# A hybrid decoder layer: the weights of the feature chunks stand at another place in their tiles

## Chip, cores, metric

One core of a Trainium2 chip runs the whole layer. The metric is the device time of one execution in microseconds.

## What is computed

One decoder layer on 256 tokens of width 1024, all in float32:

```python
u = rms_norm(x, attn_pre_norm)
q, k, v, x_lru, g_lru, gate_attn, gate_lru = split(u @ w_in)        # seven parts of 1024 columns
y_attn = moba_attention(rope(q), rope(k), v) @ w_branch_attn        # 8 heads of 128, causal
y_lru  = (rg_lru(conv4(x_lru)) * gelu(g_lru)) @ w_branch_lru        # recurrent branch, w_rg_a, w_rg_i
x = x + rms_norm((sigmoid(gate_attn) * y_attn + sigmoid(gate_lru) * y_lru) @ w_out)
x = x + rms_norm(square(relu(rms_norm(x) @ w_mlp_up)) @ w_mlp_down) # 1024 -> 4096 -> 1024
```

With 256 tokens the attention has one block of keys, so it is plain causal attention.

## The kernel before

**Every product is three matmuls.** Weights and features are split into a high part (rounded to the matmul's own 32-bit format) and a low part (what is left). A product is high x high, high x low and low x high, added up in one PSUM bank. `three` (L179) issues them: L180 multiplies the high weights with the high features, L181 the high weights with the low features, L182 the low weights with the high features. Each of them loads its weights anew.

**Weights come in 74 chunks** of 128 x 2048 numbers (1 MB), in one fixed order. `load` (L88) brings a chunk into one of three `wraw` tiles with a DMA from SyncE's queue. `split` (L104) makes the high part from it on ScalarE (L117), or on VectorE for chunks 17 to 22 (L115, `HI_ON_VECTOR`), and the low part on VectorE (L118, raw minus high). The parts go to tiles `whi` and `wlo`, three of each. `ahead` (L123) keeps the loads up to four chunks and the splits up to two chunks in front of the products; the splits have high priority in the order of their engines.

**Two kinds of chunks.** In a *feature chunk* the weights are what is loaded into TensorE (128 x 128 blocks), and the features stream past it, 256 columns at a time (all tokens). `feat_chunk` (L201) issues 2 x 8 x 3 = 48 matmuls for one; the first chunk has a function of its own (L191), and the two gate matrices of the recurrent branch have their own loop (L337). There are 48 feature chunks: chunks 0, 2, 4 and 6 (x_lru), 8 to 37 (q, k, the recurrent gates, three gate projections, the two branch projections) and 44 to 57 (up projection). In a *token product* it is the other way round: the features are loaded, and 512 columns of weights stream past. These are the chunks 1, 3, 5 and 7 (v, L233 to L235), 38 to 41 (`w_out`, L495 to L497), 42 and 43 (first 512 columns of the up projection, L602 to L604) and 58 to 73 (down projection, L495 to L497 again).

**Where the operands stand.** A `whi` or `wlo` tile has 2048 + 64 columns (`W_STEP`, L41 and L96). `weight_tiles` (L95) gives a slice of 2048 columns of it, which begins at the columns that the table `OFFSET` (L45) names: the first number is for the high part, the second for the low part, and a chunk that the table does not name begins at column 0. The table names all feature chunks and none of the token products. The tiles `gap_...` (`GAPS`, L40) only take up room. In the program as it is laid out, the tiles of the features (`xgh`, `xgl`, `xch`, `xcl`, `ath`, `atl`, `lrh`, `lrl`, `u2_12`, `u2_3`) and all of `whi` and `wlo` begin 32 columns past a multiple of 64 columns in their partition: `xgh` at byte 46208, the first `whi` at 161152, the first `wlo` at 186496. Blocks inside a tile start at multiples of 128 columns. So a slice that begins at column 0 of its tile stands at the place of the features modulo 64 columns, and one that begins at column 48 stands 48 columns past it, or 16 short of the next such place.

**The order of the work.** The four x_lru chunks and the four v chunks alternate in the opening, while the loads arrive. Then come q and k, the recurrent gates, the three gate projections (L435) with the heads of the attention stepped between them (`attention_step`, small matmuls L387 to L412), the branch projections (L461, L467), `w_out` with the post norm, the first up columns by tokens with transposes (L613), 14 feature chunks of the up projection (L626) and the down projection. Between two `feat_chunk` calls TensorE only waits for what `ahead` and the PSUM banks make it wait for.

Of the kernel before, what the change touches and what calls it, by code (L numbers as in the profile page):

```python
# [41 lines left out]

OFFSET = {c: (48, 16) for c in (*range(0, 8, 2), *range(8, 38), *range(44, 58))}  # L45


@with_exitstack
def hybrid_layer(ctx: ExitStack, tc: tile.TileContext, head_d, x_d, w_d, cst_d, gp_d, out_d):
# [45 lines left out]
    def weight_tiles(c):  # L95
        hi = whi_p.tile([P, 2048 + W_STEP], F32R, tag="whi", name=f"whi{c}")  # L96
        lo = wlo_p.tile([P, 2048 + W_STEP], F32R, tag="wlo", name=f"wlo{c}")
        h, l = OFFSET.get(c, (0, 0))
        return hi[:, h:h + 2048], lo[:, l:l + 2048]
# [637 lines left out]
```

## Time and profile before

| | |
|---|---|
| time, median of 3 runs | 442.46 us (442.3 to 617.95) |
| time of the profiled execution | 443.12 us |
| its span, first to last instruction | 441.3 us |
| busy: TensorE matmuls, weight loads | 429.0 us, 402.0 us |
| busy: VectorE, ScalarE, GpSimd | 293.1 us, 239.7 us, 20.7 us |
| mean granted TensorE clock | 0.996 of full speed |

The profile is one execution, recorded instruction by instruction. PE is TensorE's matmuls, PEld its weight loads, which run beside matmuls; DVE is VectorE, ACT ScalarE, POOL GpSimd, SP SyncE. The duration of a matmul is the time it is in flight: matmuls overlap, so the sum of durations is more than the time, and the distance between the starts of two neighbours is the better measure of their cost. L180 means line 180 of the kernel. PEclk is the share of TensorE's full clock that was granted.

### The profile page before, as it was taken

The numbers are of one execution on the slowest core, as the hardware profiler recorded it, in microseconds if no ns is written. First come the engines' busy times: TensorE is split into PE (matmuls) and PEld (weight loads), VectorE is DVE, ScalarE is ACT, GpSimd is POOL, SyncE is SP. The second block draws the span as 40 slices with busy tenths as digits, with TensorE's granted clock in tenths as the row PEclk, the third lists the DMA queues.
The fourth block names the chain that finished last, engine by engine and source line by source line (L and its number), as shares of the span: only waits on it lengthen the run. The fifth ranks groups of instructions, "written<-read, shape, count | busy, mean of one in ns | idle before, by whom it ended". The sixth has DMA issues, their size and how long they took to land.

```text
span 441.3 us, 7246 instructions
## 1 busy us (share of the span) xinstructions
PE 429.0 (97%) x3044; PEld 402.0 (91%) x3044; DVE 293.1 (66%) x353; ACT 239.7 (54%) x326; POOL 20.7 (5%) x48
## 2 busy tenths in 40 slices
PE   6989999999999999999999999999999999999994
PEld 6979999999999999999998879999999988888883
DVE  6749975779997666985688665666666644444424
ACT  7595753419977667553455566555555533333321
POOL 1000063202000000000000000000000000000000
PEclk9999999999999999999999999999999999999998
DMA  8968456655543455445567504555554555555202
GB/s 276 409 238 338 176 215 212 222 209 214 193 165 123 161 218 195 166 140 187 186 257 301 197 0 179 174 182 175 175 181 183 192 190 190 192 196 192 83 1 95
DMA packets 14576, 83.61 MB, mean 189 GB/s; under 512 B 1808, under 2 KB 2576, under 8 KB 5456
## 3 DMA queue, kind: packets, MB, share of 16 engines
q1 hardware_dynamic: 13520, 80.39, 50.7%
q0 software_dynamic: 736, 2.36, 1.6%
q8 instruction: 24, 0.39, 0.4%
q10 hardware_dynamic: 288, 0.39, 0.2%
q14 instruction: 8, 0.07, 0.0%
HBM read 81.04 MB, written 1.05 MB: 186 GB/s over the span
## 4 chain that ended last, share of the span: by engine, by line
PE 91%; DMA 5%; ACT 1%; DVE 1%; issue 0%; SPq 0%; DVEq 0%
PE mm L181 19%; PE mm L180 19%; PE mm L182 18%; PE acc L497 8%; PE acc L495 8%; PE acc L496 8%; DMA x_tok<-in_x_dram 2%; DMA wraw<-in_w_dram 1%; DMA xw_a<-in_head_dram 1%; PE up L604 1%; PE up L602 1%; PE v L233 1%; PE up L603 1%; PE v L234 1%; PE rg L181 1%; PE v L235 1%
## 5 line engine op out<-in xcount | busy, mean ns | idle before, releaser
L118 DVE TENSOR_TENSOR wlo<-wraw,whi 128x2048 fp32r<-128x2048 f32 (+2 forms) x78 | 163.6, 2099 | 88.3 <-ACT whi L117 87.9
L117 ACT CAST whi<-wraw 128x2048 fp32r<-128x2048 f32 (+2 forms) x72 | 125.2, 1739 | 95.8 <-PE acc L497 47.1
L180 PE MATMUL mm<-xgh,whi 128*128 128x256 f32 x384 | 107.7, 284 | 4.2 <-ACT xgh L171 4.2
L182 PE MATMUL mm<-xgh,wlo 128*128 128x256 f32 x384 | 106.6, 278 | 1.6 <-DVE wlo L118 1.6
L181 PE MATMUL mm<-xgl,whi 128*128 128x256 f32 x384 | 107.1, 280 | 0.0
L180 PEld LDWEIGHTS mm<-xgh,whi 128*128 128x128 f32 x384 | 72.2, 190 | 4.5 <-ACT xgh L171 4.2
L182 PEld LDWEIGHTS mm<-xgh,wlo 128*128 128x128 f32 x384 | 72.8, 189 | 1.8 <-DVE wlo L118 1.8
L181 PEld LDWEIGHTS mm<-xgl,whi 128*128 128x128 f32 x384 | 72.8, 189 | 0.5
L181 PE MATMUL mm<-u,whi 128*128 128x256 f32 x224 | 63.3, 283 | 0.0
L180 PE MATMUL mm<-u,whi 128*128 128x256 f32 x224 | 62.5, 279 | 0.0
L182 PE MATMUL mm<-u,wlo 128*128 128x256 f32 x224 | 62.4, 278 | 0.0
L497 PE MATMUL acc<-whi,rrl 128*128 128x512 f32 x128 | 49.8, 389 | 0.0
L496 PE MATMUL acc<-wlo,rrh 128*128 128x512 f32 x128 | 49.8, 389 | 0.0
L495 PE MATMUL acc<-whi,rrh 128*128 128x512 f32 x128 | 49.8, 389 | 0.0
L180 PEld LDWEIGHTS mm<-u,whi 128*128 128x128 f32 x224 | 42.1, 188 | 0.0
L182 PEld LDWEIGHTS mm<-u,wlo 128*128 128x128 f32 x224 | 42.0, 188 | 0.0
L181 PEld LDWEIGHTS mm<-u,whi 128*128 128x128 f32 x224 | 41.9, 187 | 0.0
L497 PEld LDWEIGHTS acc<-whi,rrl 128*128 128x128 f32 x128 | 24.0, 188 | 5.0
L496 PEld LDWEIGHTS acc<-wlo,rrh 128*128 128x128 f32 x128 | 24.0, 188 | 5.0
L495 PEld LDWEIGHTS acc<-whi,rrh 128*128 128x128 f32 x128 | 24.0, 188 | 4.9
L637 ACT CAST rrh<-rv 128x512 fp32r<-128x512 f32 x14 | 8.7, 621 | 34.6 <-DVE rv L636 34.6
L181 PE MATMUL mm<-atl,whi 128*128 128x256 f32 x64 | 18.1, 283 | 0.0
(197 smaller groups left out, 667.8 us busy)
## 6 DMA issues: line engine op xcount, KB each, us to landing
wraw<-in_w_dram SPq DMA_DIRECT2D x70, 1024.0 KB, 4.8
wraw<-in_w_dram SPq DMA_DIRECT2D x8, 256.0 KB, 6.1
xw_a<-in_head_dram SPq DMA_DIRECT2D x4, 256.0 KB, 4.3
wraw<-in_w_dram SPq DMA_DIRECT2D x2, 512.0 KB, 7.2
x_tok<-in_x_dram SPq DMA_DIRECT2D x1, 1024.0 KB, 10.5
gp<-in_gp_dram POOLq DMA_DIRECT2D x1, 1024.0 KB, 5.5
xw_b<-in_head_dram SPq DMA_DIRECT2D x3, 256.0 KB, 5.1
out_dram<-res ACTq DMA_DIRECT2D x2, 192.0 KB, 2.0
```

Of the source, the lines that this page charges most:

```text
L117: nc.scalar.copy(hi[:, k:(i + 1) * n], raw[:, k:(i + 1) * n])
L118: nc.vector.tensor_tensor(lo[:, s], raw[:, s], hi[:, s].bitcast(F32), ALU.subtract)
L180: nc.tensor.matmul(out, wh, xh, start=start, stop=False)
L181: nc.tensor.matmul(out, wh, xl, start=False, stop=False)
L182: nc.tensor.matmul(out, wl, xh, start=False, stop=stop)
L233: nc.tensor.matmul(banks[b], xgh[:, kb, s], hi[:, k, :], start=kb == 0, stop=False)
L234: nc.tensor.matmul(banks[b], xgh[:, kb, s], lo[:, k, :], start=False, stop=False)
L235: nc.tensor.matmul(banks[b], xgl[:, kb, s], hi[:, k, :], start=False, stop=kb == KB - 1)
L495: nc.tensor.matmul(out, xh[:, s], hi[:, hs], start=first, stop=False)
L496: nc.tensor.matmul(out, xh[:, s], lo[:, hs], start=False, stop=False)
L497: nc.tensor.matmul(out, xl[:, s], hi[:, hs], start=False, stop=last)
L637: nc.scalar.copy(hi, v)
```

## The change

The table `OFFSET` names the same chunks, with another pair of numbers: both parts of a feature chunk's weights begin at column 13 of their tiles, where the high part began at column 48 and the low part at column 16. Nothing else changes: not the tiles or their sizes, nor the instructions or their order. 13 columns are 52 bytes.

```diff
-OFFSET = {c: (48, 16) for c in (*range(0, 8, 2), *range(8, 38), *range(44, 58))}
+OFFSET = {c: (13, 13) for c in (*range(0, 8, 2), *range(8, 38), *range(44, 58))}
```

## Rows read from the trace of the kernel before

**Rows 1.** The page, part 1: busy us (share of the span) xinstructions.

```profile
PE 429.0 (97%) x3044; PEld 402.0 (91%) x3044; DVE 293.1 (66%) x353; ACT 239.7 (54%) x326; POOL 20.7 (5%) x48
```

**Rows 2.** The page, part 4: chain that ended last, by engine, by line.

```profile
PE 91%; DMA 5%; ACT 1%; DVE 1%; issue 0%; SPq 0%; DVEq 0%
PE mm L181 19%; PE mm L180 19%; PE mm L182 18%; PE acc L497 8%; PE acc L495 8%; PE acc L496 8%; DMA x_tok<-in_x_dram 2%; DMA wraw<-in_w_dram 1%; DMA xw_a<-in_head_dram 1%; PE up L604 1%; PE up L602 1%; PE v L233 1%; PE up L603 1%; PE v L234 1%; PE rg L181 1%; PE v L235 1%
```

**Rows 3.** Waits of PE: us in total, times, longest.

```profile
PE mm L180 <- ACT xgh L171: 4.2, 1, 4.2
PE mm L182 <- DVE wlo L118: 1.6, 1, 1.6
```

**Rows 4.** Windows: length, busy (xinstructions) PE, PEld, DVE, ACT, POOL; PEclk, DMA, GB/s.

```profile
57.60:112.00 54.40, 54.40 (x482) 54.40 (x481) 41.28 (x38) 27.25 (x37) 17.88 (x37) 1.00 0.61 213
112.00:125.00 13.00, 13.00 (x112) 12.88 (x111) 12.88 (x21) 12.14 (x21) 0.00 (x0) 1.00 0.49 174
125.00:130.90 5.90, 5.90 (x50) 5.87 (x49) 5.90 (x12) 5.03 (x13) 0.00 (x0) 1.00 0.53 181
...
167.00:186.10 19.10, 19.10 (x161) 19.00 (x160) 15.60 (x20) 12.48 (x20) 0.00 (x0) 1.00 0.46 166
186.10:231.70 45.60, 45.60 (x386) 45.60 (x385) 33.37 (x29) 22.12 (x18) 0.00 (x0) 1.00 0.56 200
...
273.00:347.60 74.60, 74.60 (x631) 74.60 (x630) 46.65 (x40) 39.76 (x40) 0.00 (x0) 1.00 0.53 187
```

**Rows 5.** Timeline of PE at 90 us, eleven matmuls: start us, us, instruction.

```profile
89.82 0.28 PE L182 MATMUL mm<-xgh,wlo 128*128 128x256 f32 x1
...
90.95 0.28 PE L180 MATMUL mm<-xgh,whi 128*128 128x256 f32 x1
```

**Rows 6.** Timeline of PE at 215 us, ten matmuls.

```profile
214.81 0.28 PE L181 MATMUL mm<-lrl,whi 128*128 128x256 f32 x1
...
215.88 0.28 PE L181 MATMUL mm<-lrl,whi 128*128 128x256 f32 x1
```

**Rows 7.** Lines L180 to L182: count, duration min/median/max in ns, first and last start.

```profile
L180 PE MATMUL mm<-ath,whi x64: 278/279/280, 186.2 to 208.6; 128*128 128x256 f32 x64
...
L181 PE MATMUL mm<-atl,whi x64: 281/283/285, 186.3 to 208.7; 128*128 128x256 f32 x64
...
L181 PE MATMUL rg<-xcl,whi x32: 276/276/276, 95.8 to 106.4; 128*128 128x256 f32 x32
...
L182 PE MATMUL mm<-ath,wlo x64: 278/278/279, 186.4 to 208.9; 128*128 128x256 f32 x64
```

**Rows 8.** Line L497 in the down projection, every third of its matmuls.

```profile
L497 PE MATMUL acc<-whi,rrl x128: 388/389/398, 348.1 to 434.4; 128*128 128x512 f32 x128
```

**Rows 9.** Timeline of PE, a v chunk's first matmuls, six from row to row.

```profile
46.72 0.40 PE L233 MATMUL v<-whi,xgh 128*128 128x512 f32 x1
...
47.88 0.39 PE L235 MATMUL v<-whi,xgl 128*128 128x512 f32 x1
```

**Rows 10.** Timeline of PE, the same chunk's last four matmuls.

```profile
51.28 0.39 PE L235 MATMUL v<-whi,xgl 128*128 128x512 f32 x1
...
51.96 0.39 PE L235 MATMUL v<-whi,xgl 128*128 128x512 f32 x1
```

**Rows 11.** Line L277, the convolution's taps.

```profile
L277 DVE SCALAR_TENSOR_TENSOR xc<-xlp,head,xc x24: 476/478/485, 33.7 to 57.8; 128x256 f32<-128x256 f32 x24
```

**Rows 12.** Lines L115, L117 and L118, the split.

```profile
L115 DVE CAST whi<-wraw x6: 1215/1224/1227, 90.4 to 119.0; 128x2048 fp32r<-128x2048 f32 x6
...
L117 ACT CAST whi<-wraw x72: 619/1905/1921, 10.5 to 418.6; 128x2048 fp32r<-128x2048 f32 x62, 128x512 fp32r<-128x512 f32 x8, 128x1024 fp32r<-128x1024 f32 x2
...
L118 DVE TENSOR_TENSOR wlo<-wraw,whi x78: 691/2292/2297, 11.1 to 420.5; 128x2048 fp32r<-128x2048 f32 x68, 128x512 fp32r<-128x512 f32 x8, 128x1024 fp32r<-128x1024 f32 x2
```

**Rows 13.** Waits of ACT.

```profile
ACT whi L117 <- PE mm L181: 38.8, 27, 3.8
```

**Rows 14.** Timeline of DVE at 112 us.

```profile
112.12 1.23 DVE L115 CAST whi<-wraw 128x2048 fp32r<-128x2048 f32 x1
```

## The prediction

> **What bounds the kernel now.** I read the shares of busy time first: TensorE has matmuls in flight for 97% of the span, VectorE works 66% of it and ScalarE 54% [rows 1]. A busy TensorE need not be one at its peak, so I went to the chain of waits: 91% of it is TensorE, the three matmul lines of `three` (L180 to L182) alone hold 56% [rows 2]. TensorE's own waits are two, 4.2 and 1.6 us, both in the opening [rows 3]. So nothing feeds TensorE late, and the time is the number of matmuls times the distance from the start of one to the start of the next; I call that distance the pitch.
>
> The pitch is where the change must act. Feature chunks issue 48 chunks x 48 = 2304 matmuls of 256 columns, each behind a weight load of its own. In the stretches of the trace [rows 4] about two of each count hang over the edges, so 57.6 to 112.0 us gives 54.4 us / 480 = 113.3 ns, and 186.1 to 231.7 us gives 45.6 / 384 = 118.8 ns. One by one the starts say the same: ten pitches in 1.13 us [rows 5], nine in 1.07 us [rows 6]. Shapes, instructions, places of the operands and granted clock (1.00) are equal in both. So the same program text runs at two pitches, a **lower** one of 113.3 and an **upper** one of 118.8 ns, and holds each over many chunks. The upper one rules in 125.0 to 130.9 (1 chunk), 167.0 to 186.1 (3), 186.1 to 231.7 (8) and 273.0 to 347.6 us (13): 25 chunks of the 48.
>
> The durations say which pairs suffer. Where the pitch is low, a matmul takes 276 ns whatever it multiplies; where it is high, high part by high part takes 279, high part by low features 283, low part by high features 278 [rows 7]. No engine released these matmuls late. The only thing beside each is the weight load for the next matmul, which reads the same memory. That two reads get in each other's way is my reading; the trace shows no memory.
>
> **The change, part by part.** It adds and removes no instruction, moves none and touches no queue and no wait: what each engine issues stays, in the same order. Four things could be priced differently.
>
> *The weight load beside the matmul.* Before, a matmul's features begin 16 columns behind one part and 48 behind the other; the load beside a matmul is of the high part twice out of three times, of the low part once. After, all three stand at 13 columns. The trace has no row of a weight read at such a place, so I bound it. Below: the lower pitch everywhere, which gives back 25 x 48 x (118.8 - 113.3) = 6.6 us. I see nothing to go further: the token products, whose pitch for 512 columns is 86.3 us / (127 x 3) = 226.5 ns [rows 8], come to 113.3 for 256 as well. Above: 16.5 ns of pitch per three matmuls (3 x 5.5) go with 3 + 7 + 2 = 12 ns of longer durations, a factor of 1.4; if all three pairs were like the worst one (7 x 1.4 = 9.6), the pitch would be 122.9. The mean is now 113.3 + 6600 / 2304 = 116.2, so that is 2304 x 6.7 = 15.4 us more.
>
> I take the lower end. The nearest rows are those of stages in which both parts already stand at one place, as after the change: the token products, at 0 columns. They begin with collisions, five pitches in 1.16 us, 232 ns [rows 9], and at the end of the same chunk stand at 0.68 / 3 = 227 ns [rows 10]; the 384 of the down projection stay there [rows 8]. A place common to both parts repeats one relation at every matmul, and that settles; two places alternate between two relations, and that can go round for 13 chunks. It is an argument from likeness: in the token products the weights move and the features are loaded, and the load has twice the time.
>
> The page "SBUF — State Buffer" of the Trainium skill (Specifications, and the box on cachelines) speaks against this place: it gives lines of 16 bytes and a penalty for each crossing to a new one, and 128 columns that start 13 columns in (52 bytes) touch 33 lines where 32 did before. As an estimate from that page, a weight load 1/32 longer that sets the pitch would make 113.3 into 116.8 and the time 443.1 - 6.6 + 8.1 = 444.6; no row here has a load that starts off such a line.
>
> *The split's writes.* L115 and L117 write the high part, L118 reads it and writes the low one, now at odd columns. For reads there is a row: L277 reads at shifts of 1, 2 and 3 columns and all 24 lie within 476 to 485 ns [rows 11], so nothing. For writes there is none; below nothing, above the two-fold speed of L115's copy lost (1224 to the 2292 ns of L118 [rows 12]) and half as much again on the others. I take nothing, and the cover is this: ScalarE waited 38.8 us in 27 pieces for TensorE to free a weight tile [rows 13], so the split is ahead, and VectorE is idle for 12.2 of the 45.6 us from 186.1 us on and has 13 us free in the 54.4 before 112. If the cover fails, it does so from 112 to 131 us, where VectorE works all the time [rows 4]: two of the six copies fall there, one at 112.1 us [rows 14] and the last at 119.0 [rows 12], so 2 x 1.07 = 2.1 us at most reach the path.
>
> *The first chunk*, whose split is the opening's wait [rows 3]: eight pieces of 256 columns, no more than 0.1 us either way by the spread above.
>
> *Settling.* With one place, each return from another shape (heads, transposes, token products; some 20) may cost five pitches that are 5 ns too long, as in [rows 9]: 0.5 us.
>
> **Sum:** 443.1 (profiled run) - 6.6 + 0.5 = 437.0. The median of the runs shown is 442.46, 0.66 below the profiled one, so on its scale it is 436.4; I give 437.0.
>
> **Rivals.**
> *Place does not matter, or the mix of the two pitches stays.* For it: today's two pitches come at one and the same place, so something else picks between them. That is also what follows from the skill's page "TensorE: Matmul & The Clock Gate" (Part 2, what happens when you issue a matmul): two independent read ports, so that loading the next weights takes nothing from the running matmul. Against it: the lengthening differs by pair, 7 ns beside the load of the low part and 2 to 3 beside the high one [rows 7], and these differ in place. Time: 442.5 to 443.1, with a mix shifted by a dozen chunks 439 to 446.
>
> *Everything at the upper pitch.* The other 23 chunks go up: 23 x 48 x 5.5 = 6.1 us, 449.2. For it: once in, that pattern never left by itself from 186 us to the end of a stage. Against it: it has different lengths for the two places, and one of those places is gone.
>
> *Slower: a collision at every weight load.* The load of both parts stands 13 columns on, near the 16 of today's low part, beside whose load the 283 ns stand. If every pair collides as that one does, the pitch is 122.9 and the time 443.1 + 15.4 = 458.5. It decides from a mean pitch of 116.2 + 8.85 / 2.304 = 120.0 on, where it is 2% (8.85 us). Against it: at that same 16 columns 23 chunks run at 113.3.
>
> *Faster by over 2%* would need a pitch of 116.2 - 3.8 = 112.4 everywhere, below any pitch of these chunks in the trace.
>
> **Chances.** The forecast (all at the lower pitch, 435.5 to 439) 0.38; place without effect or a mix, 0.22; all upper, up to 451, 0.13; a collision at every load, over 451, 0.25; faster than 433.6, 0.02. 2% is about what a measurement of this kernel can tell from no change. Faster by over 2% is the last case alone, 0.02; slower is the fourth, 0.25; within 2% is the rest, 0.73. The range: its lower end is the median's scale less the whole excess, 442.46 - 6.9 = 435.5; its upper end is 457, which leaves out the heavier half of the slower case (0.13) and the last case. The likeliest one's own range is 435.5 to 439.
>
> **What would show it.** Right: in 186.1 to 231.7 us' stage and in the up projection, the stretch per chunk falls from 5.70 to 5.44 us, all matmuls of L180 to L182 last 276 ns, and the token products keep 227 ns. The rows of L115, L117 and L118 keep their lengths, and TensorE's waits stay two. Wrong: three equal durations above 279 ns in all stages (collision at every load), or 279, 283 and 278 again in the same chunks (no effect), or waits of TensorE on L115 or L118 (the split's writes). The weakest step is the likeness to the token products: if one common place does not settle where the load has only one pitch of time, the forecast falls.

## The result, and the profile after

The changed kernel takes **440.33 us** (median of 5 runs, 439.65 to 440.69) against 442.46 before: a ratio of 0.9948 with a 95% interval of 0.9935 to 0.9960, 2.1 us less. That is faster by 0.5%, clear of the noise, and well within 2%. The forecast was 437.0. The profiled execution took 440.47 us with a span of 438.7.

TensorE's share and its waits, after. First its part of the page, then the chain by engine and line, then TensorE's waits (us in total, times, longest):

```profile
PE 428.0 (98%) x3044; PEld 401.3 (91%) x3044; DVE 292.8 (67%) x353; ACT 238.9 (54%) x326; POOL 21.6 (5%) x48
```

```profile
PE 97%; DMA 1%; DVE 0%; ACT 0%; issue 0%; DVEq 0%
PE mm L180 20%; PE mm L181 20%; PE mm L182 20%; PE acc L497 8%; PE acc L495 8%; PE acc L496 8%; PE v L233 2%; PE v L234 2%; PE v L235 2%; PE up L602 1%; PE up L604 1%; PE rg L181 1%; PE rg L182 1%; PE rg L180 1%; PE up L603 1%; PE s L388 1%
```

```profile
PE mm L180 <- ACT xgh L171: 4.2, 1, 4.2
```

Nothing feeds TensorE late, as in [rows 1 to 3]; the feature chunks are still what the time consists of. The wait of 1.6 us on `wlo` is absent from this execution. It is the opening's own variation: a wait of 1.8 us on the same instruction stands in the trace of the experiment with mixed places below.

The windows show what moved (columns as in [rows 4]; two matmuls of each count hang over the edges):

```profile
57.70:109.60 51.90, 51.90 (x435) 51.90 (x434) 36.93 (x36) 22.22 (x27) 16.20 (x36) 1.00 0.57 200
...
188.80:232.30 43.50, 43.50 (x386) 43.50 (x385) 32.35 (x29) 22.12 (x18) 0.00 (x0) 1.00 0.54 198
279.70:344.90 65.20, 65.20 (x578) 65.20 (x577) 43.05 (x36) 35.56 (x37) 0.00 (x0) 1.00 0.53 193
```

The branch projections went from 45.6 us [rows 4] to 43.5: 43.5 / 384 = 113.3 ns. The up projection's last 12 chunks run at 65.2 / 576 = 113.2. But the stretch from 57.7 us on, 113.3 ns before, is now at 51.9 / 433 = 119.9. The starts and durations of single matmuls say it too; timelines of PE at 90 us and at 215 us (12 matmuls each), then lines L180 to L182 in the recurrent gates (`rg`) and the first branch projection (`ath`, `atl`): count, duration min/median/max in ns, first and last start.

```profile
89.75 0.28 PE L182 MATMUL mm<-xgh,wlo 128*128 128x256 f32 x1
...
91.07 0.28 PE L181 MATMUL mm<-xgl,whi 128*128 128x256 f32 x1
```

```profile
214.79 0.28 PE L181 MATMUL mm<-lrl,whi 128*128 128x256 f32 x1
...
216.03 0.28 PE L180 MATMUL mm<-lrh,whi 128*128 128x256 f32 x1
```

```profile
L181 PE MATMUL mm<-atl,whi x64: 276/276/276, 188.9 to 210.4; 128*128 128x256 f32 x64
L181 PE MATMUL rg<-xcl,whi x32: 283/283/283, 98.3 to 109.4; 128*128 128x256 f32 x32
...
L182 PE MATMUL mm<-ath,wlo x64: 276/276/276, 189.1 to 210.5; 128*128 128x256 f32 x64
L182 PE MATMUL rg<-xch,wlo x32: 284/284/284, 98.4 to 109.6; 128*128 128x256 f32 x32
```

Eleven pitches take 1.32 us at 90 us (120.0 ns) and 1.24 us at 215 us (112.7). In [rows 5 to 7] it was the other way round: 276 ns in `rg`, 278 to 283 in the branch projection.

The sum by stretches, from the starts of the matmuls at their borders in both traces:

| stretch | before, us | after, us | after - before |
|---|---|---|---|
| opening, to chunk 8 | 52.2 | 52.1 | -0.1 |
| chunks 8 to 18 | 60.3 | 63.8 | +3.5 |
| chunks 19 to 29 with the heads | 73.7 | 72.9 | -0.8 |
| branch projections, `w_out`, first up columns | 81.3 | 79.2 | -2.1 |
| up projection, chunks 44 to 57 | 80.1 | 77.0 | -3.1 |
| the rest | 93.7 | 93.7 | 0 |

All 25 chunks at the upper pitch before now run at 113.3 ns: 6.6 us came back. But 14 chunks are at 120.0 ns: 2, 6, 8 to 18 and 44, of which all had run at 113.3. They take 14 x 48 x 6.7 ns = 4.5 us: 6.6 - 4.5 = 2.1, which is the difference of the medians. The table adds up to -2.6, the difference of the two profiled spans; its opening hides two things that nearly cancel, the missing wait of 1.6 us on the one hand, chunks 2 and 6 and a slower first chunk on the other. These 14 are the chunks that follow token products with no other work on TensorE between, and those that follow them in turn. The last v matmuls and the first of chunk 8, timeline of PE after:

```profile
51.85 0.39 PE L235 MATMUL v<-whi,xgl 128*128 128x512 f32 x1
52.07 0.28 PE L180 MATMUL mm<-xgh,whi 128*128 128x256 f32 x1
52.19 0.28 PE L181 MATMUL mm<-xgl,whi 128*128 128x256 f32 x1
52.31 0.28 PE L182 MATMUL mm<-xgh,wlo 128*128 128x256 f32 x1
52.43 0.28 PE L180 MATMUL mm<-xgh,whi 128*128 128x256 f32 x1
```

The pitch is 0.12 us from the first one on: there is no settling to see. Behind the heads there is some: in chunks 19 to 29 the 15 pitches after the first average 115 to 116 ns before they stand at 113.3, which is why chunks 19 to 29 gave back 0.8 us and not the 4 x 48 x 5.5 ns = 1.1 us of their four chunks at the upper pitch.

### The profile page after: what moved, and what is told of

It is laid out like the page before. It is cut to its first block, busy times and chain, and to the rows that moved or that the text cites. A ratio compares the mean times of both kernels' runs of the same rounds, so it can differ in the third digit from the quotient of the medians.

```text
span 438.7 us, 7246 instructions
## 1 busy us (share of the span) xinstructions
PE 428.0 (98%) x3044; PEld 401.3 (91%) x3044; DVE 292.8 (67%) x353; ACT 238.9 (54%) x326; POOL 21.6 (5%) x48
## 4 chain that ended last, share of the span: by engine, by line
PE 97%; DMA 1%; DVE 0%; ACT 0%; issue 0%; DVEq 0%
PE mm L180 20%; PE mm L181 20%; PE mm L182 20%; PE acc L497 8%; PE acc L495 8%; PE acc L496 8%; PE v L233 2%; PE v L234 2%; PE v L235 2%; PE up L602 1%; PE up L604 1%; PE rg L181 1%; PE rg L182 1%; PE rg L180 1%; PE up L603 1%; PE s L388 1%
## 5 line engine op out<-in xcount | busy, mean ns | idle before, releaser
L118 DVE TENSOR_TENSOR wlo<-wraw,whi 128x2048 fp32r<-128x2048 f32 (+2 forms) x78 | 163.6, 2100 | 85.7 <-ACT whi L117 85.7
L117 ACT CAST whi<-wraw 128x2048 fp32r<-128x2048 f32 (+2 forms) x72 | 125.3, 1741 | 90.0 <-PE acc L497 45.8
L180 PE MATMUL mm<-xgh,whi 128*128 128x256 f32 x384 | 109.2, 288 | 4.2 <-ACT xgh L171 4.2
L181 PE MATMUL mm<-xgl,whi 128*128 128x256 f32 x384 | 108.6, 283 | 0.0
L182 PE MATMUL mm<-xgh,wlo 128*128 128x256 f32 x384 | 108.6, 283 | 0.0
L180 PEld LDWEIGHTS mm<-xgh,whi 128*128 128x128 f32 x384 | 73.6, 194 | 4.5 <-ACT xgh L171 4.2
L181 PEld LDWEIGHTS mm<-xgl,whi 128*128 128x128 f32 x384 | 73.5, 191 | 0.5
L182 PEld LDWEIGHTS mm<-xgh,wlo 128*128 128x128 f32 x384 | 73.4, 191 | 0.0
L180 PE MATMUL mm<-u,whi 128*128 128x256 f32 x224 | 62.0, 277 | 0.0
L182 PE MATMUL mm<-u,wlo 128*128 128x256 f32 x224 | 62.0, 277 | 0.0
L181 PE MATMUL mm<-u,whi 128*128 128x256 f32 x224 | 61.9, 277 | 0.0
L497 PE MATMUL acc<-whi,rrl 128*128 128x512 f32 x128 | 49.8, 389 | 0.0
L180 PEld LDWEIGHTS mm<-u,whi 128*128 128x128 f32 x224 | 42.1, 188 | 0.0
L181 PEld LDWEIGHTS mm<-u,whi 128*128 128x128 f32 x224 | 42.1, 188 | 0.0
L182 PEld LDWEIGHTS mm<-u,wlo 128*128 128x128 f32 x224 | 42.1, 188 | 0.0
L497 PEld LDWEIGHTS acc<-whi,rrl 128*128 128x128 f32 x128 | 24.0, 188 | 5.0
L182 PE MATMUL mm<-lrh,wlo 128*128 128x256 f32 x64 | 17.7, 276 | 0.0
```

Of the source, the lines that this page charges most:

```text
L117: nc.scalar.copy(hi[:, k:(i + 1) * n], raw[:, k:(i + 1) * n])
L118: nc.vector.tensor_tensor(lo[:, s], raw[:, s], hi[:, s].bitcast(F32), ALU.subtract)
L180: nc.tensor.matmul(out, wh, xh, start=start, stop=False)
L181: nc.tensor.matmul(out, wh, xl, start=False, stop=False)
L182: nc.tensor.matmul(out, wl, xh, start=False, stop=stop)
L497: nc.tensor.matmul(out, xl[:, s], hi[:, hs], start=False, stop=last)
```

## The experiments

The theory formed on this (A in the expectations): for a given distance between loaded weights and streaming features there are a few patterns that hold themselves, and the way a run of chunks begins picks one. Its rivals: the stage picks (B), the pattern hangs on the whole past (C), and several on what makes a distance good. Times and ratios against the kernel before:

| run | median, us | ratio, 95% interval | pitches in its chunks, ns |
|---|---|---|---|
| changed kernel (13, 13) | 440.33 | 0.9935 to 0.9960 | 113.3, 120.0 |
| e1 (13, 13), a transpose | 437.11 | 0.9858 to 0.9888 | 113.3; 120.0 in 3 chunks |
| e2 (48, 16), a transpose | 442.62 | 0.9983 to 1.0018 | 113.3, 118.9, as before |
| e3 mixed places | 435.97 | 0.9827 to 0.9911 | 113.3 |
| e4 (0, 0) | 450.0 | 1.0156 to 1.0186 | 120.0 in all 48 |
| e5 (16, 16) | 443.12 | 0.9960 to 1.0031 | 113.3, 117.8 |
| e6 (12, 12) | 446.92 | 1.0073 to 1.0131 | 117.7 to 118.4; 123 in 3 |
| e7 (32, 32) | 448.24 | 1.0103 to 1.0161 | 118.7, 120.0 |
| e8 (48, 16), a transpose at chunk 30 | 440.17 | 0.9885 to 0.9993 | 113.3, 118.9 |
| e9 features moved by 16 | 438.07 | 0.9876 to 0.9955 | 113.3, 117.8 |
| e10 (13, 13), a short matmul | 436.56 | 0.9831 to 0.9916 | as e1 |
| e11 (48, 16), four transposes | 443.22 | 1.0002 to 1.0053 | 113.3, 118.9 |
| e12 (14, 14) | 445.66 | 1.0042 to 1.0110 | 117.8 in all 48 |

**What comes before a run of chunks: e1, e10 and e2.** One instruction more, ahead of chunk 8. Its result is not used; it takes one of the PSUM banks that the v chunks and the heads use in turn.

```diff
+    def kick(on): on and nc.tensor.transpose(at_bank("kick")[:, 0:P], ident, ident)
...
-            bank = feat_chunk(c0 + j, of(xgh), of(xgl))
+            bank = kick(c0 + j == C_Q) or feat_chunk(c0 + j, of(xgh), of(xgl))
```

Expected of e1: 

> The changed kernel (13, 13) with one 128-column transpose more on TensorE, just ahead of chunk 8 (the first of q). Theory A: for each place there are two patterns that hold themselves, and what TensorE ran just before a run of feature chunks picks one; in the changed kernel a return from 128-column float32 work gave the lower pitch (113.3 ns), a return from token products the upper one (120.0). Then chunks 8 to 18 run at 113.3 ns, 5.33 us for 47 pitches instead of 5.64; 11 x 0.32 - 0.3 = 3.2 us less, 437.2 us. Rival B: the stage picks (what the other engines and the transfers do in the first 115 us, or the distance to the tile of the features). Then the transpose changes nothing but its own 0.2 to 0.3 us: 440.6 us, 120.0 ns in chunks 8 to 18.

Expected of e2: 

> The kernel before (48, 16) with the same transpose at the same place. Theory A: in that kernel returns from transposes gave the upper pitch (118.9 ns) and returns from token products the lower one, so the same transpose does the opposite here: chunks 8 to 18 go from 113.3 to 118.9, 11 x 0.27 + 0.3 = 3.2 us more, 445.6 us. Rival B: nothing but the transpose's own 0.2 to 0.3 us, 442.7 us, 113.3 ns in chunks 8 to 18.

Measured: 437.11 us for e1, and chunks 8 to 18 at 113.3 ns, as theory A said. The stage and the instructions of the other engines are the same and the pitch is another, so the stage (B) is out for these chunks. The timeline of PE around the transpose, and the gates' line in the same trace (283 ns without the transpose):

```profile
51.07 0.39 PE L235 MATMUL v<-whi,xgl 128*128 128x512 f32 x1
51.30 0.27 PE L214 MATMUL kick<-ident 128*128 128x128 f32 x1
51.33 0.36 PE L180 MATMUL mm<-xgh,whi 128*128 128x256 f32 x1
51.53 0.28 PE L181 MATMUL mm<-xgl,whi 128*128 128x256 f32 x1
```

```profile
L181 PE MATMUL rg<-xcl,whi x32: 276/276/276, 95.1 to 105.6; 128*128 128x256 f32 x32
```

The transpose costs 0.14 us (from the last v matmul to chunk 9 it is 5.81 us, against 5.67 in the kernel before) and gives 11 chunks their lower pitch. e2 went against A's second half: 442.62 us, and chunks 9 to 18 stay at 54.3 / 480 = 113.1 ns (columns: length, busy, xmatmuls, PEclk, DMA, GB/s):

```profile
56.80:111.10 54.30, 54.30 (x482) 1.00 0.61 213
```

So a transpose does not lead into the upper pattern of the pair (48, 16); A keeps only that the entry picks, not which kind of entry picks what.

For e10 the extra instruction was a matmul of the chunks' own format:

```diff
+    def kick(on): on and nc.tensor.matmul(at_bank("kick")[:, 0:P], xgh[:, 0, 0:P], xgh[:, 0, 0:P], start=True, stop=True)
```

Expected: 

> The changed kernel with one more matmul ahead of chunk 8, as in the run with one transpose (437.1 us), but of the same format as the chunks' own (a 128-column block of the features times itself). If any break of the rhythm lets the pattern start anew, chunks 8 to 18 run at 113.3 ns and the time is 437 us; if it takes a float32 instruction, they stay at 120.0 ns, 440.5 us.

Measured: 436.56 us (two executions), chunks 9 to 18 at 54.3 / 479 = 113.4 ns:

```profile
57.30:111.60 54.30, 54.30 (x481) 1.00 0.62 213
```

A break in the rhythm is enough; it needs no float32 instruction.

**The upper pattern of the pair (48, 16): e8 and e11.** The kernel before, with one transpose ahead of chunk 30 (the edit of e1 at the call in L462, `j == 0`), and with four in its place.

Expected of e8: 

> The kernel before (48, 16) with one 128-column transpose ahead of chunk 30 (first branch projection), in the middle of its stretch at the upper pitch. If a return from a single float32 instruction lets the pattern of this pair of places start anew, chunks 30 to 37 go from 118.9 to 113.3 ns: 8 x 0.27 - 0.3 = 1.9 us less, 440.7 us. If entries after transposes lead to the upper pattern for this pair (as in chunks 21, 27 to 29 and 45), nothing changes but the transpose's own 0.2 to 0.3 us: 442.8 us.

Expected of e11: 

> The kernel before with four transposes ahead of chunk 30 instead of the one that released the upper pattern there (440.2 us). In the up projection four transposes lead into the upper pattern. If the number, that is the moment at which the chunk's first load and matmul meet, decides: chunks 30 to 37 at 118.9 ns again, 443 us. If a float32 entry as such releases and the up projection has another reason: 113.3 ns, 440.5 us.

Measured: 440.17 us with one, 443.22 with four. Lines L181 of the two traces, low part of the heads' features, first e8, then e11:

```profile
L181 PE MATMUL mm<-atl,whi x64: 276/276/283, 185.3 to 206.7; 128*128 128x256 f32 x64
```

```profile
L181 PE MATMUL mm<-atl,whi x64: 281/282/285, 186.1 to 208.6; 128*128 128x256 f32 x64
```

One transpose released eight chunks (they stay at 113.3 up to `w_out`), four did not. Of e8's two expectations the first came true, of e11's the one by which the number decides: the kind of instruction is the same, so the kind is not what picks. That the number acts through the moment at which the chunk's first load and matmul meet is a reading; no run varied that moment alone.

**Both places, each where it ran well: e3.**

```diff
-OFFSET = {c: (13, 13) for c in (*range(0, 8, 2), *range(8, 38), *range(44, 58))}
+OFFSET = {c: (13, 13) if 19 <= c < 38 or c > 44 else (48, 16)
+          for c in (*range(0, 8, 2), *range(8, 38), *range(44, 58))}
```

Expected: 

> Each run of feature chunks gets the pair of places that ran it at the lower pitch: (48, 16) for chunks 0, 2, 4, 6, 8 to 18 and 44, (13, 13) for 19 to 37 and 45 to 57. Theory A: all of them stay at the lower pitch, since what comes ahead of each run on TensorE is the same as in the kernel that ran it so: 13 chunks + chunk 44 at 0.32 us each come off the changed kernel's time, 440.4 - 4.4 = 436.0 us. Rival B (the stage picks) gives the same number. Rival C: the pattern depends on the whole past, to the nanosecond; then some run falls into an upper pitch and 437 to 440 us come out.

Measured: 435.97 us, as expected to 0.1 us, and the lowest median of all: 0.9869 of the kernel before (0.9827 to 0.9911), where the changed kernel has 0.9948. Its interval overlaps with those of e1 and e10, so it is not shown to be faster than these. Line L181 of the other kernels is line 182 here; in the up projection (`u`), the branch projection and the gates the median durations are the 276 ns of the lower pitch:

```profile
L182 PE MATMUL mm<-u,whi x224: 276/276/281, 267.5 to 343.8; 128*128 128x256 f32 x112
L182 PE MATMUL mm<-atl,whi x64: 276/276/276, 188.3 to 209.8; 128*128 128x256 f32 x64
...
L182 PE MATMUL rg<-xcl,whi x32: 276/276/276, 98.6 to 109.2; 128*128 128x256 f32 x32
```

Rival C fell: the runs of chunks behaved as in the kernel that each place came from, although what lay before them had changed. The profiled execution was the slowest of this version's four (439.67; the others 435.52 to 436.18), its matmuls waited in the opening, in chunk 4, and behind the longer wait 16 pitches were 213 ns long, while the granted clock stood at the lower of its two levels (0.50 of full speed, 1.2 GHz, from 32.2 to 35.7 us). Together that is 2.4 + 1.6 = 4.0 us, and the later chunks ran as expected in spite of it:

```profile
PE mm L183 <- DVE wlo L119: 1.8, 1, 1.8
PE mm L181 <- ACT whi L118: 0.6, 1, 0.6
```

**The distance: e4, e5, e6, e7, e12.** The changed kernel with another number in the table, (0, 0), (16, 16), (12, 12), (32, 32) and (14, 14).

Expected of (0, 0): 

> Both parts at column 0 of their tiles in the feature chunks too, the place of the features. The prediction's step, one common place settles, would give 113.3 ns nearly everywhere as at 13: 436 to 438 us. Theory A: a common place has an upper pattern of its own, which some entries fall into; whether it is the runs after token products as at 13 is open: between 436 (none) and, if its upper pitch is near 120 in all 48 chunks, 451 us. Rival D: one common place is good only because it is off the features' place, and at the features' own place every load collides: all 48 chunks above 119 ns, 449 us or more.

Expected of (16, 16): 

> Both parts at column 16, where the low part stood before. Known so far: both at 0 ran all 48 chunks at 120.0 ns (450.0 us), both at 13 ran 14 of them at 120.0 and the rest at 113.3 (440.3), and the pair (48, 16) ran 25 at 118.9. Theory A (each place has its own set of lasting patterns, the entry picks among them): 16 is near 13, so it has the lower pattern too, and the entries after float32 work find it; 113.3 ns in 30 chunks or more, 436 to 441 us. Rival E (what counts is standing off a multiple of 16 columns, 13 is good because it is odd): 120 ns everywhere as at 0, 450 us.

Expected of (12, 12): 

> Both parts at column 12: one column from 13, and a whole number of 16-byte lines (48 bytes). Theory A: the same two patterns as at 13, 113.3 and 120.0 ns, and about the same chunks in each, 438 to 442 us. Rival F (a place off the 16-byte lines costs or gives something of its own): a pitch other than 113.3 and 120.0 ns in all 48 chunks.

Expected of (32, 32): 

> Both parts at column 32, as far from the features' place as a distance modulo 64 columns can be. If the distance to the features' place is what keeps the reads apart, this is the best place: 113.3 ns in all chunks, 436 us. If places repeat sooner than every 64 columns (every 32 or 16), it is the worst, as 0: 120.0 ns everywhere, 450 us.

Expected of (14, 14): 

> Both parts at column 14, to see how wide the good place is: 12 had no chunk at 113.3 ns (446.9 us), 13 has 34 of 48 (440.3), 16 has 11 (443.1). If the place acts in steps of several columns, 14 is like 13: 440 to 441 us. If each column has a pattern of its own: any pitch from 113.3 to 120 ns, 436 to 450 us.

Measured, by windows of PE alone (length, busy, xmatmuls, PEclk, DMA, GB/s). First (0, 0) in chunks 10 to 17, the branch projections and the up projection's last 12 chunks:

```profile
63.00:109.00 46.00, 46.00 (x386) 1.00 0.57 200
191.40:237.40 46.00, 46.00 (x385) 1.00 0.56 199
285.20:354.20 69.00, 69.00 (x578) 1.00 0.51 183
```

46.0 / 384 and 69.0 / 576 are 119.8 ns (120.0 by the starts, since the windows begin and end inside a pitch): all 48 chunks are at the upper pitch, and no entry helps (rival D). (16, 16) in the first and the second of these stretches, 44.0 / 374 = 117.6 and 43.4 / 383 = 113.3:

```profile
63.00:107.00 44.00, 44.00 (x376) 1.00 0.60 207
188.10:231.50 43.40, 43.40 (x385) 1.00 0.56 202
```

and (14, 14), 46.0 / 391 = 117.6 and 45.0 / 383 = 117.5, throughout (117.8 by the starts):

```profile
63.00:109.00 46.00, 46.00 (x393) 1.00 0.57 201
190.70:235.70 45.00, 45.00 (x385) 1.00 0.56 202
```

In the same two stretches (12, 12) has 46.0 / 389 = 118.3 and 45.1 / 383 = 117.8, (32, 32) 46.0 / 384 = 119.8 and 45.5 / 383 = 118.8; two rows of each:

```profile
63.00:109.00 46.00, 46.00 (x391) 1.00 0.58 202
190.40:235.50 45.10, 45.10 (x385) 1.00 0.56 200
```

```profile
63.00:109.00 46.00, 46.00 (x386) 1.00 0.57 201
190.80:236.30 45.50, 45.50 (x385) 1.00 0.55 199
```

(16, 16) missed the expectation of 30 good chunks (12 came: 4, 19, 20 and 29 to 37; the expectation of (14, 14) counts 11) and refuted its rival, 120 ns everywhere as at 0. (12, 12) has no chunk at 113.3 and 13 next to it has 34; 12 and 16 are multiples of four columns, 13 and 14 are none, and each kind has a place with the lower pitch and one without, so that is not what makes a place good. (32, 32), the farthest, is nearly as bad as 0. Each of the columns tried has its own pitches, and the lower one, where it is found, is 113.3 ns. Theory A's expectation failed for (12, 12), which has none of the two patterns of 13. What rival F names as its sign came there, but 12 is on the 16-byte lines and 14, which is off them, has no chunk at 113.3 either, so the lines do not explain it.

**Distance, or place in the memory: e9.** The features moved instead of the weights.

```diff
-GAPS = {"const": 1, "s5": 4}
+GAPS = {"const": 7, "s5": 4, "wraw": 2}
...
-OFFSET = {c: (13, 13) for c in (*range(0, 8, 2), *range(8, 38), *range(44, 58))}
+OFFSET = {c: (0, 0) for c in (*range(0, 8, 2), *range(8, 38), *range(44, 58))}
...
-    gap(whi_p, "whi")
+    gap(wraw_p, "wraw"), gap(whi_p, "whi")
```

The features move by 48 columns and the weights by 64: the tiles of the features then begin 16 columns past a multiple of 64, those of the weights at 32 as before. So the distance is that of (16, 16) to the column, and the weights stand at the same place as in e4 modulo 64 columns, not at the same bytes, as the expectation has it.

Expected: 

> All weights at column 0 of their tiles as in the run with both at 0, but the tiles of the features begin 16 columns earlier (48 instead of 32... that is, 16 past a multiple of 64 columns, where the weights stay at 32). So the weights stand at the same bytes as in that run (all 48 chunks at 120.0 ns, 450.0 us) and 16 columns past the features as in the run with both at 16 (118 and 113.3 ns, 443.1 us). If the distance between the two reads is what counts: about 117.8 ns in chunks 4 to 18 and in the up projection, 113.3 in the branch projections, 443 us. If the place of the weights in the memory counts by itself: 120.0 ns in all chunks, 450 us. The token products are at a distance of 16 too here; their share of the time is read from their rows.

Measured: 438.07 us (eight executions, 436.88 to 441.87). The trace is of one of 441.62; what was different in those near 437 is not on record. Chunks 10 to 17, the branch projections, and the last 12 chunks of the up projection:

```profile
63.00:105.00 42.00, 42.00 (x373) 1.00 0.61 217
184.60:228.00 43.40, 43.40 (x386) 1.00 0.56 201
275.70:343.40 67.70, 67.70 (x577) 1.00 0.52 186
```

42.0 / 371 = 113.2, 43.4 / 384 = 113.0, 67.7 / 575 = 117.7: the two pitches of distance 16, and never the 120.0 that the weights' place had in e4. So the distance between what is loaded and what streams counts, and not the place of the weights alone. But the distance does not fix the mix: 20 chunks (2, 6, 8 to 18, 22 to 28) are at the lower pitch here and were at 117.8 in e5, which was not expected. For chunks 2, 6 and 8 to 18 what precedes them differs, since the token products now stand at distance 16 too and have another rhythm; that this is the reason is not shown. Line L497, the down projection, in e9 (in [rows 8] 389 ns, 348.1 to 434.4):

```profile
L497 PE MATMUL acc<-whi,rrl x128: 392/397/398, 344.0 to 432.9; 128*128 128x512 f32 x128
```

88.9 us / 381 = 233.3 ns for 226.5, 2.6 us over its 384 matmuls. The distance moves the pitch of token products as well; the v chunks of the same trace go only to 228.8 ns.

## Why the prediction was wrong

**Right.** The bound (the pitch in the feature chunks), the two pitches and their 25 chunks, the floor of 113.3 ns (no run went below it), and the 6.6 us that the 25 chunks would give back: they gave them. The split's writes at odd columns cost next to nothing: medians of 1229, 1912 and 2293 ns for L115, L117 and L118, against 1224, 1905 and 2292 in [rows 12]. The token products kept their pitch. The direction was right too.

**Wrong.** The step that failed is the one named as the weakest: "a place common to both parts repeats one relation at every matmul, and that settles". It was taken from the token products at distance 0. At that very distance the feature chunks never settle (e4, 120.0 ns in all 48), and at 14 neither (e12, 117.8). At 13 there are two lasting patterns, and runs of chunks that begin right behind token products lie in the upper one, 120.0 ns. The 4.5 us of these 14 chunks are the term that the sum lacks. With it the sum is 437.0 + 4.5 = 441.5, against 440.47 of the profiled execution; on the scale of the medians, and without the 0.5 us for settling, it is 442.46 - 6.6 + 4.5 = 440.4, against 440.33. The settling was there, but smaller, about 0.3 us in chunks 19 to 29. The forecast gave the common place one pattern, and left which pattern a run of chunks enters to a rival; e1 shows that the entry alone is worth 440.33 - 437.11 = 3.2 us. (The range's lower end takes off 6.9 us where the sum has 6.6; nothing hangs on that.)

**How the rivals fared.** "Place does not matter" fell: the times at seven places run from 440.33 to 450.0 us with the same instructions, and two of the places together give 435.97. "Everything at the upper pitch" was true of other distances (0, 12, 14, 32), not of 13. "A collision at every load" came in 14 chunks of 48, at 120.0 ns and not 122.9. I had weighed these as either-or for all chunks; the trace of before had already shown both pitches under one place, and that spoke for a mix at the new place too, with the entries of [rows 4] reshuffled. That case had 0.22 and a range of 439 to 446, which holds the time.

Two rules of the Trainium skill stood against each other there. Its page "TensorE: Matmul & The Clock Gate" (Part 2, what happens when you issue a matmul) has two independent read ports and no loss for the running matmul from the next load; here the distance of the two reads alone moves the pitch from 113.3 to 120.0 ns, so the trace disagrees. Its page "SBUF — State Buffer" (the box on cachelines) has a penalty for each crossing to a new 16-byte line; here 13, off a line, reaches the same 113.3 ns as 16, and 12, on one, does not reach it: no run here shows the penalty for a weight load.

**Open.** Which moment of entry leads to which pattern is not settled: one transpose releases the upper pattern of (48, 16) and four do not, but no run here tells why. That two reads of the memory meet is the reading that fits e9; the trace shows no memory, only the pitch. Each pattern is read from one trace per kernel; e9's times lie up to 5 us apart, so its patterns may differ from one execution to the next.

## What to carry to other kernels

Where each matmul has a weight load of its own and few columns to stream (256 here), take the pitch stage by stage, not the mean: two lasting pitches under the same shapes mean that the distance in memory between what is loaded and what streams, and the way a stage begins, are worth a scan by single columns and a single short matmul ahead of a stage. A placement is chosen per run of chunks and checked in each, since one that mends a stage can spoil the next. Do not infer a pattern at one shape from another shape at the same distance.

## What the runs showed of the hardware that was not expected

- With 256 streaming columns the pitch is 113.3 ns at best and 117.7 to 120 in the lasting bad patterns (123 in three chunks at 12), by the column distance; 12, 13 and 14 differ (117.7 to 118.4; 113.3 or 120.0; 117.8).
- A bad pattern, once entered, holds through 11 chunks (528 matmuls, 63 us) at 13. One short matmul ahead of them, of either format, keeps them out of it (e1, e10) for 0.14 us or less, and one in the middle of a bad stretch of (48, 16) ends it (e8).
- Four transposes at the same point do not end it (e11), one does (e8).
- Token products of 512 columns, 226.5 ns at distance 0, take 228.8 (v chunks) to 233.3 (down projection) at distance 16 (e9).
